# Attention values joined in one TensorE sequence with the next heads' scores, in a two-layer hybrid decoder trunk

## The chip, the core and the metric

The kernel runs on one core of a Trainium2 chip. The metric is the device time of one execution in microseconds (us), the median of several runs. The core has TensorE (PE, with its weight loads shown as PEld), VectorE (DVE), ScalarE (ACT), GpSimd (POOL) and SyncE (SP, which issues the DMAs). PE writes its results to PSUM, which has eight banks of 512 fp32 columns; the other data lie in SBUF.

## The reference

The model has two layers over 256 tokens of width 1024, all in float32. Each layer normalizes its input, projects it with one wide matrix `w_in`, and feeds three token mixers in parallel:

```python
o_mla  = mla_branch(cq, ckv, k_rope, ...)       # 8 heads, causal softmax attention
o_moba = moba_branch(mq, mk, mv, ...)           # 8 heads of 64; one block of 256, so again causal attention
o_ret  = retention_branch(rq, rk, rv, rg, ...)  # 4 heads: (q k^T * decay) v, group norm, gate
merged = (sigmoid(g_mla) * (o_mla @ w_branch_mla)
          + sigmoid(g_moba) * (o_moba @ w_branch_moba)
          + sigmoid(g_ret) * (o_ret @ w_branch_ret))
x = x + merged @ w_out
x = x + square(relu(norm(x) @ w_up)) @ w_down
```

A last normalization gives the output. With 256 tokens MoBA has one block only, so that its block selection falls away and plain causal attention is left.

## The kernel before, in words

**Projections as wide sums.** Every weight matrix comes from HBM in blocks of at most 128 x 1024 fp32 (`raw`). ACT copies a block to a rounded high part (`whi`, line 191), DVE subtracts to get the low part (`wlo`, line 193), and PE adds three products per piece (lines 212 to 214, `three`): high by high, high by low, low by high. These are the wide sums: 128 x 128 weights against 512 columns. A projection of 512 columns needs two PSUM banks (one for each 128 tokens) out of the pool `acc` of four banks (`acc_tile`), and is cut into four units of one weight block each, that is 12 wide sums a unit. All else that passes through PSUM (transposes, scores, values) takes a bank from the other pool of four, `misc` (`misc_tile`).

**Order of the work.** `prog` is a list of units in the order of a layer: ... `mv`, the gates `gmla0`, `gmla1` (four units each), `gmoba0`, `gmoba1` (four each), the branch products `bmla0`, `bmla1` (two each), `rqk`, `rv`, `rg` (four each), `bmoba0`, `bmoba1`, the gates `gret0`, `gret1`, `bret0`, `bret1`, then the output projection. `at(slot, step)` hangs a step behind a unit; `slot("gmoba0", 3)` is the place behind unit 3 of `gmoba0`. `run()` emits unit after unit with its steps. This gives the program's order. The framework's planner then reorders the instructions of each engine with a model of their times before the kernel is compiled; what it decides is fixed. A block under `tc.manual_schedule(engines={PE})` keeps the order among its own PE instructions, though others may come between them.

**Attention** (`attention`, line 429). For each head a step writes scores (MLA: line 750, full-height products; MoBA: line 382, in `together`), DVE takes masked maxima (lines 402, 405), ACT the exponentials (411), DVE normalizes (416). Two units or more later a step turns the head's probabilities on PE (line 422) and ACT copies them from PSUM (424, `probT`). `values(h0)` multiplies four heads' probabilities with their values (lines 449, 451): each product uses half the array's columns (128 x 64), two heads beside each other; the result, one bank `po` of `misc`, is split by ACT and DVE (231, 232). MoBA's scores of four heads are half the array's rows high (64 x 128), again two heads at once, and fill all four `misc` banks; retention's scores are of the same kind (`ret_scores`, line 812). Each fp32 product shows as two records in the trace.

**Places.** MLA starts at `first = slot("mv", 3)`; its scores of head h are at first+h, its turnings at first+h+2, its two groups of values at first+6 and first+10, the latter being behind unit 1 of `gmoba0`. MoBA starts at `slot("gmoba0", 3)`, with `GAP = 9`: scores of heads 0 to 3 there, turnings at +3 and +4, values at +5, and the other four heads nine units later. `moba_turn(i)` (line 770) transposes q and k for two heads, at -3, -2, +1 and +2 from MoBA's start. Retention: transposes of q and k (line 806) behind `rv` units 1 and 2, scores behind `rv` 3, `ret_values` (826 to 828) behind `rg` 2, `group_norm` behind `rg` 3, and the transposes of the result (line 866, `oret_turn`) behind `gret0` 3. The gates' results leave the sums' banks by ACT's tanh (line 481).

Of the kernel before, what the change touches and what calls it, by code (L numbers as in the profile page):

```python
# [7 lines left out]
F32 = mybir.dt.float32  # L8
# [6 lines left out]
P = 128  # L15
D = 1024
S = 256
# [10 lines left out]
MLA_H, MLA_QR, MLA_KVR, NOPE, ROPE, VD = 8, 256, 128, 64, 32, 64  # L28
QKD = NOPE + ROPE
MB_H, MB_D = 8, 64  # L30
RT_H, RT_K, RT_V = 4, 64, 128
# [97 lines left out]
def trunk(ctx: ExitStack, tc: tile.TileContext, gx, wts, consts, gfin, gn, xtok, out):  # L129


    nc = tc.nc
# [4 lines left out]
    sb = ctx.enter_context(tc.tile_pool(name="sb", bufs=1))  # L137
# [8 lines left out]
    DEC = cp.tile([P, K_END - K_DEC], F32, name="DEC")  # L146
# [55 lines left out]
    def misc_tile(name="misc"):  # L202
        return ps.tile([P, 512], F32, name=name, tag="misc", bufs=4)
# [4 lines left out]
    def t4(name):  # L208
        return sb.tile([P, 4, S], F32R, name=name, tag="t4", bufs=T4)
# [20 lines left out]
    def split_plain(src, hi, lo):  # L230
        nc.scalar.activation(hi, src, AF.Copy)
        nc.vector.tensor_sub(lo, src, hi.bitcast(F32))
# [126 lines left out]
    def rope(xv, c0, s0, t, n, h, w=None):  # L359
# [10 lines left out]
        nc.vector.tensor_sub(xv[:, :, 0, :], av[:, :, 0, :], bv[:, :, 1, :])  # L370
        nc.vector.tensor_add(xv[:, :, 1, :], av[:, :, 1, :], bv[:, :, 0, :])

    def together(parts, heads):

        with tc.manual_schedule(engines={mybir.EngineType.PE}):
            for banks, a, b in heads:
                for o, sa, sb_ in parts:
                    for j, bank in enumerate(banks):  # L380
                        rows = slice(64 * j, 64 * j + 64)
                        nc.tensor.matmul(bank[:, o], a[rows, sa], b[rows, sb_], start=True, stop=True)  # L382

    def copied_pair(pt):

# [4 lines left out]
    def attention_head(score, scale):  # L390


        got = {}

        def scores(s_ps=None):
            if s_ps is None:
                s_ps = misc_tile("ps_s")
                score(s_ps[:, 0:P], slice(0, P), slice(0, P))
                score(s_ps[:, P : 3 * P], slice(P, S), slice(0, S))
            p = sb.tile([P, 3 * P], F32, name="prob", bufs=4)  # L400
            m = small("smx")
            nc.vector.tensor_tensor_reduce(
                p[:, 0:P], s_ps[:, 0:P], mask[:, P : 2 * P], 1.0, NEG_INF, ALU.add, ALU.max, m[:, 0:1]
            )
            nc.vector.tensor_tensor_reduce(
                p[:, P : 3 * P], s_ps[:, P : 3 * P], mask, 1.0, NEG_INF, ALU.add, ALU.max, m[:, 1:2]
            )
            nc.vector.tensor_scalar(m[:, 2:4], m[:, 0:2], -scale, None, op0=ALU.mult)  # L408
            spans = ((0, P), (P, 3 * P))
            for i, (a, b) in enumerate(spans):  # L410
                nc.scalar.activation(  # L411
                    p[:, a:b], p[:, a:b], AF.Exp, bias=m[:, 2 + i : 3 + i], scale=scale, accum_out=m[:, 4 + i : 5 + i]
                )
            nc.vector.reciprocal(m[:, 6:8], m[:, 4:6])
            for i, (a, b) in enumerate(spans):
                nc.vector.tensor_scalar(p[:, a:b], p[:, a:b], m[:, 6 + i : 7 + i], None, op0=ALU.mult)
            got["p"] = p

        def turn():
            pt = misc_tile("ps_pt")  # L420
            for i, src in enumerate((0, P, 2 * P)):
                nc.tensor.transpose(pt[:, P * i : P * i + P], got["p"][:, src : src + P], ident)  # L422
            pT = sb.tile([P, 3 * P], F32, name="probT", bufs=5)
            nc.scalar.activation(pT, pt[:, : 3 * P], AF.Copy)
            return pT

        return scores, turn

    def attention(oT, score, vs, scale, first, group=None):


        pT = {}

        def turned(h, turn):
            pT[h] = turn()

        def values(h0):


            o, v = misc_tile("po"), vs()  # L440
            with tc.manual_schedule(engines={mybir.EngineType.PE}):
                for h in (h0 + 2, h0):
                    cs = slice(S * (h - h0) // 2, S * (h - h0) // 2 + S)
                    for i in range(2):
                        for j in (1, 0):
                            vh = v[i][:, VD * (h + j) : VD * (h + j) + VD]
                            dst = o[64 * j : 64 * j + 64, cs]
                            if i == 0:
                                nc.tensor.matmul(dst, vh, pT[h + j][:, 0:S], start=True, stop=False)  # L449
                            else:  # L450
                                nc.tensor.matmul(dst[:, P:S], vh, pT[h + j][:, S : 3 * P], start=False, stop=True)  # L451
            split_plain(o, *(part[:, h0 // 2 : h0 // 2 + 2, :].rearrange("p k s -> p (k s)") for part in oT))

        heads = [attention_head(lambda o, qs, ks, h=h: score(h, o, qs, ks), scale) for h in range(8)]
        for h, (scores, turn) in enumerate(heads):
            if group is None:
                at(first + h, scores)
                at(first + h + 2, lambda h=h, turn=turn: turned(h, turn))
                if h % 4 == 3:
                    at(first + h + 3, lambda h=h: values(h - 3))  # L460
        if group is None:
            return

        def four(h0):
            for h, bank in enumerate(group(h0), h0):
                heads[h][0](bank)

        for i in range(2):
            at(first + GAP * i, lambda i=i: four(4 * i))
            for h in range(4):  # L470
                at(first + GAP * i + 3 + h // 2, lambda h=4 * i + h: turned(h, heads[h][1]))
            at(first + GAP * i + 5, lambda i=i: values(4 * i))

    def gates(l, key, xn):

# [84 lines left out]
    def at(slot, step):  # L560
        steps.setdefault(slot, []).append(step)

    def slot(key, j):
        return [k for k, _ in prog].index((key, j))
# [9 lines left out]
    def layer(l, xn, before):  # L574

        c0 = []
        c, mla, mqkv, rqkv = {}, {}, {}, {}
# [164 lines left out]
        omlaT, omobaT, oretT = [], [], []  # L742
# [3 lines left out]
        first = slot("mv", 3)  # L746
        at(first, lambda: omlaT.extend((t4("omlah"), t4("omlal"))))

        def mla_score(h, o, qs, ks):
            nc.tensor.matmul(o, mla["Q"][:, h, qs], mla["K"][:, h, ks], start=True, stop=True)  # L750

        attention(
            omlaT, mla_score,
            lambda: mla["v"], QKD**-0.5, first,
        )

        th_moba = gates(l, "gmoba", xn)
        merged, mT = {}, []  # L760
        branch(l, "bmla", omlaT, th_mla, merged)
        first = slot("gmoba0", 3)
        at(first, lambda: omobaT.extend((t4("omobah"), t4("omobal"))))
        qkT = {}

# [16 lines left out]

        for i in range(4):
            at(first + 4 * (i // 2) - 3 + i % 2, lambda i=i: moba_turn(i))
        attention(omobaT, None, lambda: mqkv["mv"], MB_D**-0.5, first, moba_scores)

# [11 lines left out]
        rT, or_ps, aT, rg, oret = [], [], {}, {}, []  # L800
# [11 lines left out]
        def ret_scores():  # L812
            banks = [misc_tile("ps_r") for _ in range(RT_H)][::-1]
            together(
                ((slice(0, S), slice(0, P), slice(0, S)), (slice(S, 3 * P), slice(P, S), slice(P, S))),
                [(banks[2 * i : 2 * i + 2], rT[i][1], rT[i][0]) for i in range(2)],
            )
            for h in range(RT_H):
                aT[h] = sb.tile([P, 3 * P], F32, name="retA", tag="prob", bufs=4)
                nc.vector.tensor_mul(aT[h], banks[h][:, : 3 * P], DEC[:, 384 * h : 384 * h + 384])  # L820

        def ret_values(h):
            if h == 0:
                or_ps.extend(misc_tile("por") for _ in range(NT))
            rv, cs = rqkv["rv"], slice(RT_V * h, RT_V * h + RT_V)
            nc.tensor.matmul(or_ps[0][:, cs], aT[h][:, 0:P], rv[0][:, cs], start=True, stop=True)
            nc.tensor.matmul(or_ps[1][:, cs], aT[h][:, P:S], rv[0][:, cs], start=True, stop=False)
            nc.tensor.matmul(or_ps[1][:, cs], aT[h][:, S : 3 * P], rv[1][:, cs], start=False, stop=True)
# [85 lines left out]
        branch(l, "bret", oretT, th_ret, merged, between)  # L914
        for i in range(2):
            at(slot("rv", 1 + i), lambda i=i: ret_turn(i))
        at(slot("rv", 3), ret_scores)
        for h in range(RT_H):
            at(slot("rg", 2), lambda h=h: ret_values(h))
        at(slot("rg", 3), group_norm)  # L920
        for i in range(2):
            at(slot("gret0", 3), lambda i=i: oret_turn(i))
# [169 lines left out]
        for t in range(NT):  # L1092
# [3 lines left out]
            for half in range(2):  # L1096
                cs = slice(512 * half, 512 * half + 512)
# [7 lines left out]
            cs = slice(0, 320)  # L1105
            nc.scalar.activation(y[:, cs], y[:, cs], AF.Copy, scale=r)
            nc.scalar.dma_start(out[:, t, cs], y[:, cs])
            cs = slice(320, D)
# [18 lines left out]
    for l in range(L):  # L1127
        xn, before = layer(l, xn, before)
# [4 lines left out]
FIRST = 4  # L1133
WHOLE = 1
AHEAD = 1
GAP = 9
T4 = 9


# [73 lines left out]
```

## Time and profile before

| | us |
|---|---|
| median of 3 runs (840.47 to 840.8) | 840.68 |
| the profiled execution | 840.62 |
| its span on the core | 838.8 |
| PE busy | 832.1 |
| DVE busy | 577.7 |
| ACT busy | 491.1 |
| POOL busy | 41.6 |

The span is the time from the first to the last instruction of the profiled execution. Busy times are sums over instructions and can overlap in time between engines. A row of the timeline gives the start in us from the span's beginning, the duration, the engine, the line of the kernel, the operation, the tiles written and read, the array shape (128\*64 is 128 rows by 64 columns) with the moving operand's shape, and how many instructions were merged into the row. On PE the durations overlap, as matmuls are pipelined: what counts is the step from one start to the next. The two layers lie at about 0 to 420 us and 420 to 839 us; the attention part of layer 0 runs from about 60 to 170 us.

### The profile page before, as it was taken

What the parts mean: (1) busy time and instruction counts of PE and PEld (TensorE: products, weight loads), DVE (VectorE), ACT (ScalarE), POOL (GpSimd) and SP (SyncE); (2) the same over time, 40 slices, a digit from 0 to 9 for tenths busy, and PEclk for the clock granted to TensorE, in tenths of its full rate; (3) what the DMA queues carried; (4) which work ended last, traced back from release to release, by engine and by line L of the source; (5) the groups of instructions that cost most, each with busy time, mean ns of one, the idle gap of its engine ahead of it and who ended that gap; (6) DMA issues with size and microseconds to landing.
All of it is one profiled execution on the core that took longest, in us unless ns stands there. A gap on an engine that the chain in (4) does not pass through costs nothing.

```text
span 838.8 us, 11982 instructions
## 1 busy us (share of the span) xinstructions
PE 832.1 (99%) x4342; PEld 702.0 (84%) x4342; DVE 577.7 (69%) x1088; ACT 491.1 (59%) x860; POOL 41.6 (5%) x45
## 2 busy tenths in 40 slices
PE   9999999999999999999999999999999999999997
PEld 7888877888888888888888887888888888888886
DVE  6887568596787666666589865675968766666663
ACT  7857666445555555555677666564455555555552
POOL 0000000040030000000000000001301200000000
PEclk9999999999999999999999999999999999999999
DMA  9865544536457566665367545454565656666641
GB/s 341 273 206 184 175 135 147 161 130 215 144 180 228 193 193 187 195 190 187 117 205 222 175 135 174 150 158 146 148 209 160 215 177 197 200 187 194 194 129 51
DMA packets 43115, 151.09 MB, mean 180 GB/s; under 512 B 4912, under 2 KB 5936, under 8 KB 43056
## 3 DMA queue, kind: packets, MB, share of 16 engines
q1 hardware_dynamic: 42480, 149.66, 56.6%
q8 instruction: 34, 0.56, 0.3%
q10 hardware_dynamic: 576, 0.67, 0.2%
q14 instruction: 25, 0.20, 0.1%
HBM read 149.26 MB, written 1.05 MB: 179 GB/s over the span
## 4 chain that ended last, share of the span: by engine, by line
PE 99%; DVE 0%; ACT 0%; issue 0%; DVEq 0%
PE acc L212 20%; PE acc L214 20%; PE acc L213 20%; PE pup L988 13%; PE pup L990 7%; PE acc L938 5%; PE ps_pt L422 1%; PE ps_s L750 1%; PE po L449 1%; PE ps_s L382 1%; PE acc L643 0%; PE pqk L770 0%; PE acc L644 0%; PE acc L646 0%; PE warm L554 0%; PE po L451 0%
## 5 line engine op out<-in xcount | busy, mean ns | idle before, releaser
L193 DVE TENSOR_TENSOR wlo<-raw,whi 128x1024 fp32r<-128x1024 f32 (+4 forms) x287 | 338.2, 1185 | 201.2 <-ACT whi L191 147.4
L191 ACT ACTIVATE whi<-raw 128x1024 fp32r<-128x1024 f32 (+4 forms) x287 | 291.9, 1023 | 182.4 <-PE acc L214 103.7
L212 PE MATMUL acc<-whi,xs 128*128 128x512 f32 (+1 forms) x384 | 151.9, 397 | 0.0
L213 PE MATMUL acc<-wlo,xs 128*128 128x512 f32 (+1 forms) x384 | 150.5, 392 | 0.0
L214 PE MATMUL acc<-whi,xs 128*128 128x512 f32 (+1 forms) x384 | 149.5, 390 | 0.0
L988 PE MATMUL pup<-xs,whi 128*128 128x512 f32 x496 | 121.5, 390 | 0.0
L988 PEld LDWEIGHTS pup<-xs,whi 128*128 128x128 f32 x496 | 91.9, 188 | 18.3
L212 PE MATMUL acc<-whi,sq 128*128 128x512 f32 x256 | 100.1, 391 | 0.0
L213 PE MATMUL acc<-wlo,sq 128*128 128x512 f32 x256 | 99.9, 390 | 0.0
L214 PE MATMUL acc<-whi,sq 128*128 128x512 f32 x256 | 98.8, 389 | 0.0
L212 PEld LDWEIGHTS acc<-whi,xs 128*128 128x128 f32 x384 | 72.1, 188 | 15.2 <-issue 1.3
L214 PEld LDWEIGHTS acc<-whi,xs 128*128 128x128 f32 x384 | 72.1, 188 | 14.4
L213 PEld LDWEIGHTS acc<-wlo,xs 128*128 128x128 f32 x384 | 72.2, 188 | 13.4
L990 PE MATMUL pup<-xs,wlo 128*128 128x256 f32 x496 | 68.8, 283 | 0.0
L990 PEld LDWEIGHTS pup<-xs,wlo 128*128 128x128 f32 x496 | 65.7, 191 | 3.1
L999 ACT ACTIVATE relu<-relu 128x256 f32<-128x256 f32 x64 | 25.5, 408 | 54.7 <-DVE relu L998 54.7
L214 PEld LDWEIGHTS acc<-whi,sq 128*128 128x128 f32 x256 | 48.1, 188 | 10.2
L212 PEld LDWEIGHTS acc<-whi,sq 128*128 128x128 f32 x256 | 48.2, 188 | 9.2
L213 PEld LDWEIGHTS acc<-wlo,sq 128*128 128x128 f32 x256 | 48.2, 188 | 8.9
L411 ACT ACTIVATE prob<-prob,smx 128x128 f32<-128x128 f32 x64 | 28.4, 446 | 15.5 <-DVE smx L408 15.1
L938 PE MATMUL acc<-mT,whi 128*128 128x512 f32 (+1 forms) x144 | 35.3, 372 | 0.0
L996 ACT COPY relu<-pup 128x256 f32<-128x256 f32 x62 | 22.3, 365 | 15.7 <-PE pup L990 15.2
(246 smaller groups left out, 1005.8 us busy)
## 6 DMA issues: line engine op xcount, KB each, us to landing
raw<-wts SPq DMA_DIRECT2D x264, 512.0 KB, 4.1
raw<-wts SPq DMA_DIRECT2D x6, 464.0 KB, 8.2
raw<-wts SPq DMA_DIRECT2D x4, 416.0 KB, 3.2
xrow<-xtok SPq DMA_DIRECT2D x4, 256.0 KB, 8.1
gn<-gn SPq DMA_DIRECT2D x2, 512.0 KB, 4.1
raw<-wts SPq DMA_DIRECT2D x3, 256.0 KB, 4.2
DEC<-consts SPq DMA_DIRECT2D x1, 768.0 KB, 6.2
y<-y SPq DMA_DIRECT2D x2, 352.0 KB, 2.6
```

The lines of the kernel that those rows point to most:

```text
L191: nc.scalar.activation(hi[:, cs], raw[:, cs], AF.Copy)
L193: nc.vector.tensor_sub(lo[:, cs], raw[:, cs], hi[:, cs].bitcast(F32))
L212: nc.tensor.matmul(o, ah, bh, start=start, stop=False)
L213: nc.tensor.matmul(o, ah, bl, start=False, stop=False)
L214: nc.tensor.matmul(o, al, bh, start=False, stop=stop)
L382: nc.tensor.matmul(bank[:, o], a[rows, sa], b[rows, sb_], start=True, stop=True)
L411: nc.scalar.activation(p[:, a:b], p[:, a:b], AF.Exp, bias=m[:, 2 + i : 3 + i], scale=scale, accum_out=m[:, 4 + i : 5 + i])
L938: nc.tensor.matmul(o, a, b, start=half == 0 and i == 0, stop=4 * half + n == KD and i == len(jobs) - 1)
L988: nc.tensor.matmul(u, w, xm.both(k), start=k == 0, stop=False)
L990: nc.tensor.matmul(u[:, 0:S], w, xm.k(k)[0], start=False, stop=k == KD - 1)
L996: nc.scalar.copy(s, u[:, S : 2 * S])
L999: nc.scalar.activation(s, s, AF.Square)
```

## The change

It touches the places where PE changes between the full array and its halves. `values` and `ret_scores` now return the part that isn't PE's (the split of the result, the decay products) as a function, and a new helper runs the PE parts of several jobs under one `manual_schedule`, then the rest:

```diff
+    def in_a_row(*jobs):
+        with tc.manual_schedule(engines={mybir.EngineType.PE}):
+            rest = [job() for job in jobs]
+        for job in rest:
+            job()
...
-        def values(h0):
-            o, v = misc_tile("po"), vs()
+        def values(h0, bank=acc_tile):
+            o, v = bank("po"), vs()
...
-            split_plain(o, *(part[:, h0 // 2 : h0 // 2 + 2, :].rearrange("p k s -> p (k s)") for part in oT))
+            dst = (part[:, h0 // 2 : h0 // 2 + 2, :].rearrange("p k s -> p (k s)") for part in oT)
+            return lambda: split_plain(o, *dst)
...
+            at(first + 6, lambda: in_a_row(lambda: values(0, misc_tile)))
+            return lambda: values(4)
...
+        at(first, lambda: in_a_row(former, lambda: four(0)))
+        at(first + GAP, lambda: in_a_row(lambda: values(0), lambda: four(4)))
         for i in range(2):
-            at(first + GAP * i, lambda i=i: four(4 * i))
             for h in range(4):
                 at(first + GAP * i + 3 + h // 2, lambda h=4 * i + h: turned(h, heads[h][1]))
-            at(first + GAP * i + 5, lambda i=i: values(4 * i))
+        return lambda: values(4)
...
-        first = slot("gmoba0", 3)
+        first = slot("gmoba0", 1)
...
-        attention(omobaT, None, lambda: mqkv["mv"], MB_D**-0.5, first, moba_scores)
+        moba_last = attention(omobaT, None, lambda: mqkv["mv"], MB_D**-0.5, first, moba_scores, mla_last)
...
-                [(banks[2 * i : 2 * i + 2], rT[i][1], rT[i][0]) for i in range(2)],
+                [(banks[2 * i : 2 * i + 2], rT[i][1], rT[i][0]) for i in (1, 0)],
...
-        at(slot("rv", 3), ret_scores)
+        at(slot("rg", 0), lambda: in_a_row(ret_scores, moba_last))
         for h in range(RT_H):
-            at(slot("rg", 2), lambda h=h: ret_values(h))
+            at(slot("rg", 3), lambda h=h: ret_values(h))
...
-GAP = 9
+GAP = 8
```

So each layer has three joined groups. MLA's values of heads 4 to 7 come directly before MoBA's scores of heads 0 to 3, behind `gmoba0` unit 1. MoBA's values of heads 0 to 3 come directly before its scores of heads 4 to 7, behind `bmla0` unit 1. Retention's scores come directly before MoBA's values of heads 4 to 7, behind `rg` unit 0. The scores in these groups fill all four `misc` banks, and the values in them take their bank from `acc`, the sums' pool. MLA's values of heads 0 to 3 stay alone and in `misc`. With MoBA's start, the four `moba_turn` steps stand two units earlier than before (behind `gmla1` units 2 and 3 and `gmoba0` units 2 and 3). Retention's scores stand one unit later, and so do its values. The number and shape of all matmuls stay the same.

More of the change, by code (lines that the diff above doesn't have):

```diff
@@ L371, in rope @@
         nc.vector.tensor_add(xv[:, :, 1, :], av[:, :, 1, :], bv[:, :, 0, :])
-    def together(parts, heads):
[L377 to L382, printed above, removed]
+    def in_a_row(*jobs):
[3 more added lines that the diff above has]
+            job()
+    def together(parts, heads):
+        for banks, a, b in heads:
+            for o, sa, sb_ in parts:
+                for j, bank in enumerate(banks):
+                    rows = slice(64 * j, 64 * j + 64)
+                    nc.tensor.matmul(bank[:, o], a[rows, sa], b[rows, sb_], start=True, stop=True)
     def copied_pair(pt):
@@ L427, in attention_head, with attention @@
         return scores, turn
-    def attention(oT, score, vs, scale, first, group=None):
+    def attention(oT, score, vs, scale, first, group=None, former=None):
         pT = {}
@@ L435, in turned @@
             pT[h] = turn()
-        def values(h0):
-            o, v = misc_tile("po"), vs()
[L441 to L451, printed above, removed]
-            split_plain(o, *(part[:, h0 // 2 : h0 // 2 + 2, :].rearrange("p k s -> p (k s)") for part in oT))
+        def values(h0, bank=acc_tile):
+            o, v = bank("po"), vs()
+            for h in (h0 + 2, h0):
+                cs = slice(S * (h - h0) // 2, S * (h - h0) // 2 + S)
+                for i in range(2):
+                    for j in (1, 0):
+                        vh = v[i][:, VD * (h + j) : VD * (h + j) + VD]
+                        dst = o[64 * j : 64 * j + 64, cs]
+                        if i == 0:
+                            nc.tensor.matmul(dst, vh, pT[h + j][:, 0:S], start=True, stop=False)
+                        else:
+                            nc.tensor.matmul(dst[:, P:S], vh, pT[h + j][:, S : 3 * P], start=False, stop=True)
+            dst = (part[:, h0 // 2 : h0 // 2 + 2, :].rearrange("p k s -> p (k s)") for part in oT)
+            return lambda: split_plain(o, *dst)
@@ L454, in attention @@
         heads = [attention_head(lambda o, qs, ks, h=h: score(h, o, qs, ks), scale) for h in range(8)]
-        for h, (scores, turn) in enumerate(heads):
-            if group is None:
+        if group is None:
+            for h, (scores, turn) in enumerate(heads):
                 at(first + h, scores)
                 at(first + h + 2, lambda h=h, turn=turn: turned(h, turn))
[L459 to L462, printed above, removed]
+            at(first + 6, lambda: in_a_row(lambda: values(0, misc_tile)))
+            return lambda: values(4)
@@ L464, in four, with rest @@
         def four(h0):
-            for h, bank in enumerate(group(h0), h0):
-                heads[h][0](bank)
+            banks = group(h0)
+            def rest():
+                for h, bank in enumerate(banks, h0):
+                    heads[h][0](bank)
+            return rest
+        at(first, lambda: in_a_row(former, lambda: four(0)))
+        at(first + GAP, lambda: in_a_row(lambda: values(0), lambda: four(4)))
         for i in range(2):
-            at(first + GAP * i, lambda i=i: four(4 * i))
@@ L750, in mla_score @@
             nc.tensor.matmul(o, mla["Q"][:, h, qs], mla["K"][:, h, ks], start=True, stop=True)
[L752 to L755, printed above, removed]
+        mla_last = attention(omlaT, mla_score, lambda: mla["v"], QKD**-0.5, first)
         th_moba = gates(l, "gmoba", xn)
@@ L815, in ret_scores, with rest @@
                 ((slice(0, S), slice(0, P), slice(0, S)), (slice(S, 3 * P), slice(P, S), slice(P, S))),
-                [(banks[2 * i : 2 * i + 2], rT[i][1], rT[i][0]) for i in range(2)],
+                [(banks[2 * i : 2 * i + 2], rT[i][1], rT[i][0]) for i in (1, 0)],
             )
-            for h in range(RT_H):
-                aT[h] = sb.tile([P, 3 * P], F32, name="retA", tag="prob", bufs=4)
-                nc.vector.tensor_mul(aT[h], banks[h][:, : 3 * P], DEC[:, 384 * h : 384 * h + 384])
+            def rest():
+                for h in range(RT_H):
+                    aT[h] = sb.tile([P, 3 * P], F32, name="retA", tag="prob", bufs=4)
+                    nc.vector.tensor_mul(aT[h], banks[h][:, : 3 * P], DEC[:, 384 * h : 384 * h + 384])
+            return rest
         def ret_values(h):
```

## The prediction

> **What bounds the kernel now.** First the page's head and the view of waits.
>
> ```profile
> span 838.8 us, 11982 instructions
> PE 832.1 (99%) x4342; PEld 702.0 (84%) x4342; DVE 577.7 (69%) x1088; ACT 491.1 (59%) x860; POOL 41.6 (5%) x45
> PE warm L554 <- PEq L1206: 0.8, 1, 0.8
> ACT whi L191 <- PE acc L214: 103.7, 86, 2.8
> ```
>
> The span is TensorE's own work from end to end. In the view of waits PE has one entry, 0.8 us at the start; ACT instead waits 103.7 us for PE before it may split the next weights (L191), so the weights are ahead of the sums. Nothing is to be won from DMA, DVE or ACT here; what can change the time is what PE itself spends, or a wait that PE gets. The profiled execution took 840.62 us, 1.82 us of it outside the span; the median of the three runs is 840.68. My sums start from 840.62.
>
> What PE spends beside its streams shows in the timeline, in the steps from one start to the next. Here is one group of values (L449, L451) between wide sums; columns are start, duration, engine, line.
>
> ```profile
> 125.44 0.39 PE L212 MATMUL acc<-whi,omlah 128*128 128x512 f32 x1
> 125.67 0.39 PE L213 MATMUL acc<-wlo,omlah 128*128 128x512 f32 x1
> 125.99 0.65 PE L449 MATMUL po<-probT,mv 128*64 128x256 f32 x4
> 126.47 0.39 PE L451 MATMUL po<-probT,mv 128*64 128x128 f32 x4
> 126.69 0.60 PE L449 MATMUL po<-probT,mv 128*64 128x256 f32 x4
> 127.12 0.39 PE L451 MATMUL po<-probT,mv 128*64 128x128 f32 x4
> 127.44 0.50 PE L214 MATMUL acc<-whi,omlal 128*128 128x512 f32 x1
> 127.78 0.40 PE L212 MATMUL acc<-whi,omlah 128*128 128x512 f32 x1
> ```
>
> A wide sum steps by 0.23 (125.44 to 125.67). The values run in a half-width array (128*64), two at a time: undisturbed, four long ones step by 0.43 (126.69 to 127.12) and four short ones by 0.22 (126.47 to 126.69), so the group's work is 1.30. From 125.67 to 127.78 pass 2.11; less two sums (0.46) and 1.30, **0.35 us** is lost at the two changes of array shape. Step by step: going in, 0.09 before the values start (0.32 for 0.23) and 0.05 in their first four (0.48 for 0.43); coming out, 0.10 after the last four (0.32 for 0.22) and 0.11 in the first wide sum (0.34 for 0.23).
>
> Scores of four heads (half-height, 64*128) between wide sums, then a place where values, transposes and half a group of scores stand together:
>
> ```profile
> 130.97 0.39 PE L214 MATMUL acc<-whi,xs 128*128 128x512 f32 x1
> 131.29 1.58 PE L382 MATMUL ps_s<-qkT 64*128 64x128 f32 x16
> 132.80 0.50 PE L212 MATMUL acc<-whi,xs 128*128 128x512 f32 x1
> 133.13 0.40 PE L213 MATMUL acc<-wlo,xs 128*128 128x512 f32 x1
> ```
>
> ```profile
> 104.50 0.39 PE L214 MATMUL acc<-whi,xs 128*128 128x512 f32 x1
> 104.81 0.65 PE L449 MATMUL po<-probT,vml 128*64 128x256 f32 x4
> ```
>
> ```profile
> 106.27 0.44 PE L770 MATMUL pqk<-K,mq 128*128 128x128 f32 x2
> 106.54 0.38 PE L770 MATMUL pqk<-K,mk 128*128 128x128 f32 x2
> 106.85 0.93 PE L382 MATMUL ps_s<-qkT 64*128 64x128 f32 x8
> 107.71 0.50 PE L212 MATMUL acc<-whi,xs 128*128 128x512 f32 x1
> 108.04 0.40 PE L213 MATMUL acc<-wlo,xs 128*128 128x512 f32 x1
> ```
>
> ```profile
> 111.58 0.93 PE L382 MATMUL ps_s<-qkT 64*128 64x128 f32 x8
> ```
>
> The 16 scores stream as much as the 16 values (eight of 128 and eight of 256 columns, in pairs), 1.30. From 130.97 to 133.13 is 2.16, less 0.46 and 1.30: **0.40**, that is 0.09 in, 0.10 in the first pair, 0.10 and 0.11 out. At 104.50 to 108.04, 3.54 less 0.46, 1.30, four transposes at 0.11 and half the scores (0.65) leaves **0.69**. (The three left-out rows of the values, between 104.81 and 106.27, have the steps of the group above.) The other half of those scores stands apart at 111.58, with the next transposes (L770) behind it. When transposes come after a narrow group, the second part of the exit is 0.05 (0.27 for two at 106.27, which alone take 0.22).
>
> **The change, part by part.**
>
> *Narrow groups in a row.* Before, each layer after its first four MLA heads has: MLA's second values with half of MoBA's first scores, 0.69; the other half, 0.09+0.10+0.10+0.05 = 0.34; MoBA's first values, 0.35; its second scores, 0.40; its second values with retention's transposes behind, 0.09+0.05+0.10+0.05 = 0.29; retention's scores (L382 too, priced as the other four-head group), 0.40. Sum 2.47. After, three groups are left, each in, across, out. No trace row has a direct step from 128*64 to 64*128. Its bounds: 0, if the array takes the new shape without emptying; 0.41, as if a wide sum still stood between (0.10+0.11 out, 0.09+0.10 in). I take 0.20, the exit's 0.10 and the first pair's 0.10, since the step from full-width transposes into scores (106.54 to 106.85) shows the same 0.09 as from wide sums: what empties doesn't depend on what comes. From scores to values it is 0.10+0.05 = 0.15. So: 0.09+0.05+0.20+0.10+0.11 = 0.55, twice; 0.09+0.10+0.15+0.10+0.11 = 0.55. Sum 1.65, a gain of 0.82 a layer, **1.64 us** in two. With the crossing at nothing it would be 2.74, with it at its full price 0.4.
>
> The Trainium skill, "TensorEngine Tiling (Array Packing)", Key Properties, says that changing the tiling mode, and not only the tile, drains the TensorE. The rows agree, with 0.09 to 0.10 at each change; by that rule the crossing isn't free, and the gain is below the 2.74 that a free one gives.
>
> *Transposes that lose their neighbours* (L770, L806) now stand alone between wide sums, at most four more places a layer. The price of such a place is in the next fence: from 99.15 to 100.38 is 1.23, less 0.46 and seven transposes at 0.11 leaves nothing. I take nothing; at most 0.05 each, 0.4 in all.
>
> *Values in the sums' banks.* This adds a wait. Here is the place in layer 0 where MLA's last head is turned; PE first, then ACT.
>
> ```profile
> 97.56 0.39 PE L214 MATMUL acc<-whi,xs 128*128 128x512 f32 x1
> ```
>
> ```profile
> 99.15 0.39 PE L212 MATMUL acc<-whi,xs 128*128 128x512 f32 x1
> 99.38 0.49 PE L422 MATMUL ps_pt<-K,prob 128*128 128x128 f32 x3
> 99.71 0.38 PE L770 MATMUL pqk<-K,mq 128*128 128x128 f32 x2
> 99.92 0.38 PE L770 MATMUL pqk<-K,mk 128*128 128x128 f32 x2
> 100.06 0.47 PE L213 MATMUL acc<-wlo,xs 128*128 128x512 f32 x1
> 100.38 0.39 PE L214 MATMUL acc<-whi,xs 128*128 128x512 f32 x1
> ```
>
> ```profile
> 97.31 1.37 ACT L481 ACTIVATE th<-acc,half 128x512 f32<-128x512 f32 x2 [0.98 <-PE acc L214]
> 98.57 1.05 ACT L191 ACTIVATE whi<-raw 128x1024 fp32r<-128x1024 f32 x1
> 99.91 0.49 ACT L424 ACTIVATE probT<-ps_pt 128x384 f32<-128x384 f32 x1 [0.28 <-PE ps_pt L422]
> ```
>
> The tanh pair (L481) shows that gmoba0's sums ended with the one at 97.56; from there on they are gmoba1's. MLA's values(4) stand in the program inside gmoba0, behind its second unit, but ran at 104.81, 7 us into gmoba1. The transposes of q and k at 99.71 had had their inputs for long, and yet ran only behind the turning that precedes them in the program: tiles of one set of banks are given out in program order. If that holds for the sums' banks, gmoba1 may not begin until these values have taken theirs. So PE will run out at 97.79, turn head 7 (0.33, to 98.12) and wait for the copy L424: 0.49 behind the tanh pair (98.68) ends at 99.17, 1.1 late; behind the weights' split as well (99.62) it ends at 100.11, 2.0 late. I take **1.5**, less the 0.09 on entry that it covers: 1.4. Behind the waiting values stand MoBA's scores and all of gmoba1, so nothing hides it. The same place in layer 1:
>
> ```profile
> 510.71 0.49 PE L422 MATMUL ps_pt<-K,prob 128*128 128x128 f32 x3
> 512.63 0.39 PE L212 MATMUL acc<-whi,xs 128*128 128x512 f32 x1
> ```
>
> ```profile
> 516.15 0.65 PE L449 MATMUL po<-probT,vml 128*64 128x256 f32 x4
> ```
>
> Here the last head is turned 1.92 before gmoba1's first sum (512.63), and 0.33+0.49 and a start fit in: no wait. The other two joined groups take their banks six and eleven units behind the scores on which they hang. Six units of 12 sums at 0.23 are 16.6 us; from the second half of the scores to their values, 111.58 to 125.99, it now takes 14.4. The work that hides them is these sums, and I cost them at nothing; were that cover gone, the price is again one copy, 1 to 2 us.
>
> The Trainium skill, "TensorE: Matmul & The Clock Gate", Architectural detail, says that ScalarE's queue is strictly first in, first out. By that the copy can't pass the tanh pair or the weights, as the ACT rows agree; a queue that let it pass would take most of the 1.5 away.
>
> *Retention one unit later, GAP 8, MoBA's start two units earlier.* The instructions are the same; no DMA is issued in a moved step, and SP's and POOL's order stays. What is late next is retention's result:
>
> ```profile
> 186.22 0.74 DVE L857 SCALAR_TENSOR_TENSOR oret<-rgb,half,oret 128x512 f32<-128x512 f32 x1
> 192.97 1.03 PE L866 MATMUL pot<-K,oret 128*128 128x128 f32 x8
> ```
>
> Ready at 186.96 and turned at 192.97: 6.0 of room for a shift of 2.7. Nothing.
>
> Sum: 840.62 - 1.64 + 1.4 = **840.4**.
>
> **The rivals.**
>
> *No wait* (values find their copy ready, or the sums' banks aren't in program order): 840.62 - 1.64 = 839.0, and 837.9 with a free crossing. For it: layer 1's row, and that the moved L770 push gmoba0's end back by 0.9. Against: 99.38 lies 1.6 behind 97.79.
>
> *Slower: gmoba1's sums held in both layers.* If head 7's turning itself, not only its copy, is planned late, PE idles for part of the way from the sums' end to the old place of the values: 97.79 to 104.81 (7.0) and 512.63 to 516.15 (3.5). Half of that is 5.3: 840.62 + 5.3 - 1.64 = 844.3. It decides from 3.3 us of waiting on. Against it: before the copy L424 ACT sat idle 0.28 us, waiting for the turning alone; on the chip the data are there as soon as PE turns them.
>
> *The change doesn't do what it says:* sums slip in between values and scores, as they did between the halves at 106.85 and 111.58. Each crossing then costs 0.41; the gain falls to 0.4 and the wait stays: 841.6.
>
> **How the numbers follow.** Forecast (one wait in layer 0) 0.38, 840.4, by itself 838.9 (free crossing, wait of 1.1) to 842.1 (full price, 2.0); no wait 0.36; held in both layers 0.18; torn apart 0.08. The bound of 0.2% is 1.68 us, about what a measurement can tell from no change. Faster by more: the part of "no wait" whose crossing is below 0.20, 0.22, and 0.04 of the forecast with its least wait: 0.26. Slower by more: all of the third and a little of the fourth, 0.19. Between them 0.55. The range goes from "no wait" with a free crossing, 837.9, to 843.0, short of the held case's middle.
>
> **What would show it.** In the profile after: 128*64 rows followed at once by 64*128 rows at two places a layer, and the reverse at one; the step across near 0.2; PE's list of waits with one entry for probT of 1 to 2 us near 98 us and none near 512; no idle PE around 120 and 160. The forecast is wrong if PE waits at a second place, if gmoba1's sums start ahead of the joined group, or if the crossing isn't near 0.2.

## The result, and the profile after

| | before | after |
|---|---|---|
| median, us (range, runs) | 840.57 (840.1 to 841.04, 19) | 838.97 (838.65 to 839.74, 19) |
| the profiled execution | 840.62 | 839.34 |
| its span | 838.8 | 837.5 |
| PE busy | 832.1 | 830.7 |

The ratio is 0.9981, with a 95% interval of 0.9975 to 0.9988: 1.6 us or 0.19% faster. The interval excludes a ratio of 1, so the gain is real; it takes in the 0.2% that the prediction names as its bound, so whether the gain passes that isn't decided. The forecast was 840.4, and the rival "no wait" gave 839.0. The head of the page after, then the first PE entry and the ACT entry of its view of waits:

```profile
span 837.5 us, 11975 instructions
...
PE 830.7 (99%) x4342; PEld 702.9 (84%) x4342; DVE 577.0 (69%) x1088; ACT 490.0 (59%) x860; POOL 42.0 (5%) x45
```

```profile
PE warm L567 <- PEq L1220: 0.8, 1, 0.8
ACT whi L191 <- PE acc L214: 101.9, 84, 3.8
```

PE still fills the span, its busy time is 1.4 us less, and the view lists no new wait of PE. The first joined group of layer 0, in PE's timeline (start, duration, engine, line):

```profile
98.15 0.49 PE L429 MATMUL ps_pt<-K,prob 128*128 128x128 f32 x3
98.40 0.48 PE L212 MATMUL acc<-whi,xs 128*128 128x512 f32 x1
98.72 0.39 PE L213 MATMUL acc<-wlo,xs 128*128 128x512 f32 x1
98.94 0.40 PE L214 MATMUL acc<-whi,xs 128*128 128x512 f32 x1
99.47 0.65 PE L456 MATMUL po<-probT,vml 128*64 128x256 f32 x4
99.95 0.39 PE L458 MATMUL po<-probT,vml 128*64 128x128 f32 x4
100.17 0.60 PE L456 MATMUL po<-probT,vml 128*64 128x256 f32 x4
100.61 0.39 PE L458 MATMUL po<-probT,vml 128*64 128x128 f32 x4
100.92 1.58 PE L389 MATMUL ps_s<-qkT 64*128 64x128 f32 x16
102.43 0.50 PE L212 MATMUL acc<-whi,xs 128*128 128x512 f32 x1
102.77 0.39 PE L213 MATMUL acc<-wlo,xs 128*128 128x512 f32 x1
```

The values that ran at 104.81 now run at 99.47, directly ahead of gmoba1's first sum at 102.43. Values and scores stand in a row. Across, the last four values step by 0.31 (100.61 to 100.92) where 0.22 is their work, so 0.09; the scores step by 1.51, 0.21 more than their streams, of which 0.10 is the exit: **0.20 for the crossing**. Ahead of the values the last sum steps by 0.53 in place of 0.32: **0.21 of waiting** in addition to the change of shape. ACT's timeline at the same place shows for what:

```profile
98.35 0.69 ACT L494 ACTIVATE th<-acc,half 128x512 f32<-128x512 f32 x1 [0.98 <-PE acc L214]
98.94 0.48 ACT L431 ACTIVATE probT<-ps_pt 128x384 f32<-128x384 f32 x1
99.38 0.69 ACT L494 ACTIVATE th<-acc,half 128x512 f32<-128x512 f32 x1
```

The copy ends at 99.42, and the values start 0.05 later. It stands between the two tanh, not behind them. The same place in layer 1:

```profile
512.44 0.39 PE L214 MATMUL acc<-whi,xs 128*128 128x512 f32 x1
512.76 0.65 PE L456 MATMUL po<-probT,vml 128*64 128x256 f32 x4
```

A step of 0.32, so no wait. Last, PE at retention's scores with MoBA's last values in layer 0:

```profile
160.37 1.58 PE L389 MATMUL ps_r<-qkT 64*128 64x256 f32 x16
161.87 0.65 PE L456 MATMUL po<-probT,mv 128*64 128x256 f32 x4
162.35 0.39 PE L458 MATMUL po<-probT,mv 128*64 128x128 f32 x4
```

From scores to values: 1.50, that is the 1.30 of the streams, 0.10 in the first pair and 0.10 of the crossing; then 0.48 in the first four values for 0.43. The crossing costs 0.15.

**Where the time came from.** For every PE step I take the undisturbed step of its shape off (0.227 for a wide sum, 0.109 for a transpose, 0.109 or 0.216 for a narrow pair) and add up what is left, in the profiled execution of each kernel: over 58 to 185 us (layer 0's attention) and 484 to 600 us (layer 1's). What stands there for before holds the changes of shape, waits and other small losses; the differences count (taken before rounding).

| kernel | layer 0, us | layer 1, us | sum, less before's | median of the runs |
|---|---|---|---|---|
| before | 5.25 | 4.31 | | 840.57 to 840.73 |
| after | 4.65 | 3.51 | -1.40 | 838.97 |
| cross3 | 5.68 | 4.66 | +0.77 | 841.45 |
| misc_bank | 6.01 | 5.05 | +1.49 | 842.23 |
| unjoined | 5.19 | 4.61 | +0.23 | 840.94 |
| first_join | 4.95 | 3.80 | -0.82 | 839.74 |
| early | 6.31 | 3.49 | +0.23 | 840.75 |
| late | 4.49 | 3.51 | -1.56 | 839.10 |
| acc_only | 6.20 | 4.05 | +0.68 | 841.37 |
| ret_later | 5.25 | 4.31 | 0.00 | 840.76 |
| eight_both | 3.95 | 3.06 | -2.56 | 838.01 |
| eight_both_late | 4.01 | 2.97 | -2.59 | 837.84 |

Layer 1 gained 0.80 and layer 0 0.60; with the wait of 0.21 taken out, layer 0 gained 0.81.

### The profile page after: what moved, and what is told of

It reads as the page before. It is cut to its first block, busy times and chain, and to the rows that moved or that the text cites. A ratio compares the mean times of both kernels' runs of the same rounds, so it can differ in the third digit from the quotient of the medians.

```text
span 837.5 us, 11975 instructions
## 1 busy us (share of the span) xinstructions
PE 830.7 (99%) x4342; PEld 702.9 (84%) x4342; DVE 577.0 (69%) x1088; ACT 490.0 (59%) x860; POOL 42.0 (5%) x45
## 3 DMA queue, kind: packets, MB, share of 16 engines
HBM read 149.26 MB, written 1.05 MB: 179 GB/s over the span
## 4 chain that ended last, share of the span: by engine, by line
PE 99%; ACT 0%; DVE 0%; issue 0%; DVEq 0%
PE acc L212 20%; PE acc L213 20%; PE acc L214 20%; PE pup L1002 13%; PE pup L1004 7%; PE acc L952 5%; PE ps_s L763 1%; PE ps_pt L429 1%; PE po L456 1%; PE ps_s L389 1%; PE acc L656 1%; PE acc L657 0%; PE acc L659 0%; PE warm L567 0%; PE po L458 0%; PE pqk L780 0%
```

## The experiments

Theory: the gain is the price of the changes of array shape, group by group, as summed in the prediction; against it stands one wait, for the copy of MLA's last head, whose size depends on where the planner puts the turning and the copy. Rivals: the gain comes from the places or the banks; the wait is never more than it was here; or the retention shift matters. Each run was timed beside the kernel before on the same chip.

**cross3: the shape changes three times in a group.**

```diff
-            rest = [job() for job in jobs]
+            jobs = [job() for job in jobs]
+            for job in jobs:
+                next(job)
+            rest = [next(job) for job in jobs]
```

Each job yields after its first half, so that values and scores alternate.

> The changed kernel, but in each of the six joined groups values and scores alternate in halves, so that PE changes shape between them three times and not once; banks, places and products stay. Theory (the gain is the price of the shape changes, 0.20 us from values to scores and 0.15 back): 6 x 0.35 = 2.1 us more than the changed kernel's 838.97, so 841.1, a little slower than the kernel before. Rival (the gain comes from the freed bank and from scores that are not torn apart, and shape changes are cheap between narrow groups): as the changed kernel, 838.8 to 839.2.

Measured: 841.45 (840.94 to 841.86), ratio to before 1.0009 [1.0, 1.0018]. PE's timeline of the first group:

```profile
99.06 0.65 PE L457 MATMUL po<-probT,vml 128*64 128x256 f32 x4
99.54 0.39 PE L459 MATMUL po<-probT,vml 128*64 128x128 f32 x4
99.86 0.93 PE L390 MATMUL ps_s<-qkT 64*128 64x128 f32 x8
100.71 0.65 PE L457 MATMUL po<-probT,vml 128*64 128x256 f32 x4
...
102.37 0.50 PE L212 MATMUL acc<-whi,xs 128*128 128x512 f32 x1
```

Half the scores take 0.85 for streams of 0.65; the group lasts 3.31 (99.06 to 102.37) where the kernel after needs 2.96 (99.47 to 102.43). That is 0.35 for one crossing more each way, as 0.20 + 0.15 say, and 1.05 for three groups; the table has 1.03 and 1.15 a layer. The theory holds: the same instructions at the same places lose the whole gain, and by the table 0.77 more, through the order inside the groups alone.

**misc_bank: the values back in the other set of banks.**

```diff
-        def values(h0, bank=acc_tile):
+        def values(h0, bank=misc_tile):
```

> The changed kernel, but the joined groups' values take their bank from the transposes' and scores' pool again, as before the change. Theory (five tiles in four banks: the last score bank must wait for the values' split, so sums slip in between, and the 0.2 us wait in layer 0 goes): two more exits and entries of 0.40 and one of 0.20 a layer, 2.0 - 0.2 = 1.8 us more than 838.97, so 840.8. Rival (the joined program order gives the gain, whatever the bank): 838.8 to 839.2.

Measured: 842.23 (841.79 to 842.49), 1.0018 [1.0009, 1.0027]. PE's timeline:

```profile
105.49 1.14 PE L389 MATMUL ps_s<-qkT 64*128 64x128 f32 x10
106.56 0.50 PE L214 MATMUL acc<-whi,xs 128*128 128x512 f32 x1
...
111.14 0.92 PE L389 MATMUL ps_s<-qkT 64*128 64x128 f32 x6
111.98 0.44 PE L780 MATMUL pqk<-K,mq 128*128 128x128 f32 x2
```

The four scores need all four banks, of which the values now hold one, and break after five products of eight. The mechanism is the expected one, the price 1.4 us higher than expected, and the rows tell why: 1.07 and 0.84, less 0.20 in each for the changes of shape, make 1.51 where 16 records together take 1.30. The tear falls inside a pair: five products (ten records) take 0.87, the time of six in pairs (0.22, 0.43 and 0.22), and the other three take 0.64, that of four (0.65). That is 0.2 for each tear, 0.8 for the four in two layers. The other 0.6 stays open; by the table, where misc_bank lies 2.89 above the kernel after, 0.3 of it is in the attention parts.

**unjoined: same places, same banks, no common row.**

```diff
-        at(first, lambda: in_a_row(former, lambda: four(0)))
+        at(first, lambda: in_a_row(former))
+        at(first, lambda: in_a_row(lambda: four(0)))
```

and the same for the two other groups.

> The steps stand at the same places as in the kernel after the change, and the values use the same banks, but values and scores are no longer kept in one row: each of them is a row of its own. Theory (the gain comes from standing in a row alone): in the order that results, the first scores of a layer are torn (5 products, 3 sums, the values, the other 3 in layer 0; 1, then 4, 14 sums, the values, 3 in layer 1), one sum slips in ahead of retention's scores, and the middle group stays whole. By the steps of the kernels measured so far each further way out and in costs 0.35 to 0.40, a crossing 0.20 less than that, and each score that loses its partner 0.1: about +0.7 in layer 0 and +1.0 in layer 1, median 840.4 to 841.0. Rival (the places or the banks bring the gain, not the row): 838.8 to 839.2.

Measured: 840.94 (840.44 to 841.17), 1.0002 [0.9994, 1.0011]: nothing of the gain is left. In the table layer 0 loses 0.54 on the kernel after and layer 1 1.10. PE's timeline of the first group of layer 0, and of retention's scores:

```profile
98.61 1.14 PE L389 MATMUL ps_s<-qkT 64*128 64x128 f32 x10
...
100.58 0.65 PE L456 MATMUL po<-probT,vml 128*64 128x256 f32 x4
...
102.03 0.92 PE L389 MATMUL ps_s<-qkT 64*128 64x128 f32 x6
```

```profile
159.28 0.50 PE L212 MATMUL acc<-whi,xs 128*128 128x512 f32 x1
159.71 1.58 PE L389 MATMUL ps_r<-qkT 64*128 64x256 f32 x16
```

The scores are torn around the values, with three sums between the first part and the values. At retention's scores the values now come first, and one sum stands between: it steps by 0.43 in place of 0.23 (159.28 to 159.71), beside the 0.10 of exit ahead of it and the 0.10 in the first pair, so 0.40 for the way across. The middle group, which the planner left whole (values at 121.69, scores at 123.14), costs what it does in the kernel after. So the gain comes from standing in one row, and where nothing pins the row, the planner parts two groups of three.

**first_join: the first group of each layer alone.**

```diff
-        at(first + GAP, lambda: in_a_row(lambda: values(0), lambda: four(4)))
+        at(first + 7, lambda: in_a_row(lambda: values(0, misc_tile)))
+        at(first + 11, lambda: in_a_row(lambda: four(4)))
+        at(first + 16, lambda: in_a_row(lambda: values(4, misc_tile)))
```

with the turnings of heads 4 to 7 and retention's steps back where they were.

> Only the first joined group of each layer is kept (MLA's last values with MoBA's first scores); MoBA's other values and scores and retention's scores stand apart again, with their tiles in the other set of banks, as in the kernel before. Theory (every group has its own price): this group costs 0.69 + 0.34 apart and 0.55 joined, so it saves 0.48 a layer, 0.96 in two; the wait in layer 0 costs 0.2: 840.57 - 0.96 + 0.2 = 839.8. The two groups left out are then worth 0.8 to 0.9 together. Rival (all the gain is in the first group, which was torn before): 838.9 to 839.2. Rival (this group wins nothing, because the wait eats it): 840.4 to 840.8.

Measured: 839.74 (839.48 to 840.41), 0.9989 [0.998, 0.9998]. In the table layer 1 gains 0.51 (0.48 by the sum) and layer 0 0.31 (0.48 less a wait of 0.2). The terms add: this group is worth a little over half, the two others the rest.

**early: the case that the prediction priced.** MoBA's start one unit earlier, so that nothing stands between the last turning and the values.

```diff
-        first = slot("gmoba0", 1)
+        first = slot("gmoba0", 0)
...
-GAP = 8
+GAP = 9
```

> MoBA's start, with MLA's last values, stands one unit earlier (behind gmoba0's first unit), GAP is 9; nothing else is changed. In layer 0 the last MLA head is then turned directly ahead of its values, with no sum between; in the kernel after the change three sums stand there (98.15 turned, 99.47 values). This is the case that the prediction priced at 1.1 to 2.0 us. Theory (the wait is the time from the turning to the end of ACT's copy, less the sums that stand between): turned and copied took 98.15 to 99.42 in the kernel after the change, 1.27 us, of which the turning itself fills 0.33; so PE waits at least 0.9 us, and 1.5 to 2.0 if a tanh pair of 1.37 us stands ahead of the copy on ACT. Median 838.97 - 0.21 + 0.9 to 2.0 = 839.7 to 840.8; layer 1, where seven sums stand between, without a wait. Rival (ACT takes the copy at once wherever the turning stands, and a wait on it costs 0.2 at most): 838.8 to 839.1, and the step from turning to values below 0.6 us.

Measured: 840.75 (840.59 to 841.22), 1.0001 [0.9992, 1.001]. The view of PE's waits, then PE and ACT in the timeline:

```profile
PE po L456 <- ACT probT L431: 1.8, 1, 1.8
```

```profile
98.55 0.49 PE L429 MATMUL ps_pt<-K,prob 128*128 128x128 f32 x3
100.82 0.65 PE L456 MATMUL po<-probT,vml 128*64 128x256 f32 x4 [1.78 <-ACT probT L431]
```

```profile
98.07 1.37 ACT L494 ACTIVATE th<-acc,half 128x512 f32<-128x512 f32 x2 [0.98 <-PE acc L214]
99.34 1.05 ACT L191 ACTIVATE whi<-raw 128x1024 fp32r<-128x1024 f32 x1
100.29 0.48 ACT L431 ACTIVATE probT<-ps_pt 128x384 f32<-128x384 f32 x1
```

Here is the prediction's wait, at its upper bound: PE is out of work at 98.88 (98.55 and 0.33 of turning) and starts again at 100.82, 1.94 later, with the copy behind the tanh pair and behind the weights' split. It eats the whole gain. The rival, that such a wait costs 0.2 at most, falls. The copy waited behind two instructions which it doesn't need, though its input was there from about 99.04 on (98.55 and 0.49). This agrees with the Trainium skill, "TensorE: Matmul & The Clock Gate", Architectural detail, which has ScalarE's queue strictly first in, first out. The ACT rows in the prediction didn't test it: there the copy still waited 0.28 for its input after the split had ended.

**late: three units later instead.** MoBA's start, with MLA's last values, stands three units later than in the kernel after: `first = slot("gmoba1", 0)` and `GAP = 7`.

> The changed kernel with MoBA's start three units later (behind unit 0 of gmoba1, GAP 7), so that the values' bank comes behind those of gmoba1. Theory (values that take a sums' bank must go ahead of the next sums, and this alone makes PE wait 0.2 us in layer 0): the joined group stands 20 and more sums behind the last turning, the wait is gone, 838.8. Rival (that wait has another cause, or the later start is late for what follows): 838.97 or more, a wait elsewhere.

Measured: 839.10 (838.46 to 839.46), 0.998 [0.9971, 0.9989]. In the trace the wait is gone (layer 0: 4.49 after 4.65, and a step of 0.32 into the values, 103.81 to 104.13); against 838.97 the medians can't tell such a difference, and by them it is a draw.

**acc_only: the kernel before, with MLA's second values in the sums' banks.**

```diff
-                    at(first + h + 3, lambda h=h: values(h - 3))
+                    at(first + h + 3, lambda h=h: values(h - 3, misc_tile if h == 3 else acc_tile))
```

> The kernel before with one edit: MLA's second values go into a bank of the sums' set in place of the other set. Theory (banks of a set are given out in program order): these values move from 104.81 to the first sums of gmoba1, near 100, behind the first half of MoBA's scores, although nothing in their place in the program is changed. By the measured steps the crossing from scores to values saves about 0.08 in layer 0 and, where the scores of four heads stay whole, 0.28 in layer 1; a wait for the copy of the last head adds 0 to 1.0 in layer 0. Median 840.2 to 841.3. Rival (the values run where their place in the other stream of work puts them, whatever the bank): they stay near 104.8 and nothing moves, 840.57.

Measured: 841.37 (840.68 to 841.84), 1.0007 [0.9998, 1.0016]. PE's timeline:

```profile
100.19 0.93 PE L382 MATMUL ps_s<-qkT 64*128 64x128 f32 x8 [1.00 <-ACT qkT L387]
101.04 0.65 PE L449 MATMUL po<-probT,vml 128*64 128x256 f32 x4
...
102.50 0.50 PE L212 MATMUL acc<-whi,xs 128*128 128x512 f32 x1
```

The values move from 104.81 to 101.04, directly ahead of gmoba1's first sum, though their place in the program is as before: the bank alone pulls them there. The order of the banks, on which the prediction's wait rested, is shown by this. The wait was another than expected: 1.00 us for the transposed q and k (qkT), since the scores came forward along with the values. Layer 1 gained 0.26 (0.28 by the sum). The median lies 0.07 above the expected range. Between the layers (400 to 484 us), which the edit doesn't touch, PE's steps hold 0.54 more in this execution, at one place; ACT first, then PE:

```profile
439.27 1.06 ACT L191 ACTIVATE whi<-raw 128x1024 fp32r<-128x1024 f32 x1 [2.71 <-DMA raw<-wts]
```

```profile
440.88 0.50 PE L212 MATMUL acc<-whi,xs 128*128 128x512 f32 x1 [0.26 <-ACT c L590]
```

A weight block came late, ACT's next work (L590) stood behind its split, and PE waited for that. It isn't part of the effect: this execution is the slowest of the eleven (841.84), and the median lies 0.68 above that of before, as the table has it without this stretch.

**ret_later: the retention shift alone, on the kernel before.**

```diff
-        at(slot("rv", 3), ret_scores)
+        at(slot("rg", 0), ret_scores)
...
-            at(slot("rg", 2), lambda h=h: ret_values(h))
+            at(slot("rg", 3), lambda h=h: ret_values(h))
```

> The kernel before with the retention edit alone: its scores and its values one unit later, nothing joined. Theory (6.0 us of room before its result is turned, and the same groups between the same sums): no change, 840.3 to 841.0. Rival (retention's chain of VectorE work is late for the transposes that turn its result, and part of what the joining wins is lost there): a wait of PE for oret, up to 2 us, in each layer, 841.0 to 844.

Measured: 840.76 (840.02 to 840.9), 0.9998 [0.9989, 1.0007]; the table's two entries are those of before. No change.

**eight_both: all eight heads' values in one stretch.** MLA's first four heads and MoBA's first four wait for the other four, so that one way in and out and one crossing a layer fall away; `probT` gets eight buffers for it.

```diff
+        def both():
+            rests = [values(4), values(0)]
+            return lambda: [r() for r in rests]
...
-        at(first + GAP, lambda: in_a_row(lambda: values(0), lambda: four(4)))
+        at(first + GAP, lambda: in_a_row(lambda: four(4)))
...
-        return lambda: values(4)
+        return both
```

> The changed kernel with all eight heads' values in one stretch: MLA's first four go into the first joined group, MoBA's first four into the last (probT has 8 buffers, both results in the sums' banks). Theory (price per shape change): MLA's values alone, 0.29 a layer, go; MoBA's second scores alone 0.40 instead of 0.55 with values; no wait in layer 0, as eight sums stand between the turning and the values: 2 x 0.44 + 0.2 = 1.1 us less than 838.97, so 837.9. Rival (two of four sums' banks for values make the sums wait): over 838.97, PE waits behind the first joined group.

Measured: 838.01 (837.57 to 838.44), 0.9968 [0.9955, 0.998], 0.96 below the kernel after. In the table layer 1 gains 0.45 on the kernel after (0.44 by the sum) and layer 0 0.70 (0.64 with its wait). PE's timeline within MoBA's eight values, behind retention's scores:

```profile
160.81 0.60 PE L456 MATMUL po<-probT,mv 128*64 128x256 f32 x4
161.24 0.39 PE L458 MATMUL po<-probT,mv 128*64 128x128 f32 x4
161.46 0.60 PE L456 MATMUL po<-probT,mv 128*64 128x256 f32 x4
```

From the first group of four to the second (161.24 to 161.46) the step is 0.22, a plain stream: values behind values change no shape and cost nothing beside their work.

**eight_both_late: the two together.** eight_both with MoBA's start of late, which is three units later than in eight_both, not one as the expectation has it.

> The version with all eight heads' values in one stretch (838.01), with MoBA's start one unit later (GAP 7), so that the last MLA head is turned some twenty sums ahead of its values in both layers. Theory: no wait for a copy is left, and the stretches are the same; the version before it already showed next to none, so 837.8 to 838.1. Rival (the buffers that are held one unit longer make another wait): over 838.4.

Measured: 837.84 (837.57 to 838.09), 0.9965 [0.9952, 0.9979]. It is the fastest version that was run, and is not to be told from eight_both.

## Why the prediction was right or wrong

**The narrow groups (1.64 us): right.** The crossing that no row of before showed was taken at 0.20 and measured 0.20 (bounds 0 and 0.41), the reverse 0.15 for 0.15. Layer 1, where PE got no wait, gained 0.80 for 0.82. The middle group of layer 0 (starts at 121.28, 122.73 and 124.24) and the three groups of layer 1 show the same steps. cross3 gives the price of the crossing, first_join that of one group, unjoined shows that the row is the cause. "Torn apart" (841.6) didn't occur in the kernel after; where it was brought about it cost 840.94 and 842.23.

The Trainium skill, "TensorEngine Tiling (Array Packing)", Key Properties, has the TensorE drain at a change of the tiling mode. The trace agrees: 0.09 of the 0.20 is time ahead of the first score with no wait listed.

**The wait in layer 0 (1.4 net): the mis-sized term.** It measured 0.21. Its place, its cause and the order of the banks were as told: the values stand ahead of gmoba1's first sum, and wait for the copy of head 7. Two steps of the prediction failed in the size. "PE will run out at 97.79, turn head 7": the turning was taken to stand behind gmoba0's last sum, and in the kernel after it stands three sums ahead of it (98.15; the last sum starts at 98.94). And "0.49 behind the tanh pair": the copy stood between the two tanh and ended at 99.42, behind the first alone. Both are choices of the planner, which orders the whole program anew; the prediction kept the order of before around the moved steps. Where the planner does leave the turning last (early), the wait is 1.94, within the predicted 1.1 to 2.0. With 0.21 in place of 1.4 the sum reads 840.62 - 1.64 + 0.21 = 839.2, beside 839.34 for the profiled execution and 838.97 for the median. So the forecast itself was 1.4 too high, and of the signs that it named one didn't come: PE's list of waits has no entry for probT.

**Layer 1 without a wait: right** (a step of 0.32).

**Transposes alone, and the retention shift, at nothing: right.** In the kernel after retention's result is ready at 188.42 and turned at 192.50:

```profile
187.68 0.74 DVE L871 SCALAR_TENSOR_TENSOR oret<-rgb,half,oret 128x512 f32<-128x512 f32 x1
```

```profile
192.50 1.03 PE L880 MATMUL pot<-K,oret 128*128 128x128 f32 x8
```

4.1 of the 6.0 us of room are left. Of the transposes, layer 1's 0.80 for 0.82 leaves 0.02 for them.

**The rivals.** "Held in both layers" (844.3) didn't come about: PE waits for a copy, not for a planned time. "No wait" at 839.0 gave the number, but only in part for its reasons. The moved transposes of q and k do stand ahead of gmoba0's end now (at 90.51 and 93.36), and its last sum starts 1.38 later than before (98.94 for 97.56). But the wait is there, and what nearly covers it is also that the turning stands 1.23 earlier (98.15 for 99.38) and the copy between the two tanh, which no rival named. The result lies in the stated range because the range took in this rival. What decided between it and the forecast, 1.4 us apart, was mainly where the planner put one turning and one copy; the profile before couldn't show that, and the two chances, 0.36 and 0.38, were nearly even for it.

## What to carry to other kernels

Price each change of array shape from the steps between starts (here 0.14 to 0.21 a side with wide products, 0.15 to 0.20 across), count the changes before and after, and expect the gain to hold only if the order is pinned: a single sum between two narrow groups (0.40 for the way across, unjoined) or a tear inside a pair (0.2, misc_bank) gives it back. A tile in a pool that is given out in program order ties its users to that order: take it from another pool, and its work can move although its step doesn't (acc_only). Where a framework reorders the program, the size of a wait that hangs on "what stands between" is known only from the new order: keep both ends, and weigh them evenly.

## What was not expected of the hardware

A product that loses its partner costs the pair's time: 16 score records took 1.30 together and 1.51 in two parts of ten and six (misc_bank), with the changes of shape taken off both. And one copy of 0.48 us became 1.94 us of PE idle (early) because 2.4 us of other work of ACT, begun 0.5 us before the turning, stood ahead of it, while ACT was busy for only 58% of the span.
